# State-space decay: exponents from products with a selecting operand, or loaded from DRAM onto all partitions

## The chip, the cores and the metric

One NeuronCore of a Trainium2 chip runs the whole kernel. The metric is the device time of one execution in microseconds (us); the median of several runs counts. Five engines work side by side and wait for each other by semaphores: PE (TensorE, matrix products and transposes into PSUM banks), DVE (VectorE), ACT (ScalarE), POOL (GpSimd) and SP (SyncE, which here only issues DMAs). All data is float32; "fp32r" is the same width in the form that TensorE takes for its rounded products.

## The reference

One inference step of a hybrid decoder layer: a sliding-window attention branch and a Mamba-2 state-space (SSD) branch side by side, an output projection, and a squared-ReLU MLP. There are 1024 prompt tokens with 16 meta tokens ahead of them, and 8 sample sequences of 4 tokens. What matters here is the decay inside the SSD scan (8 heads, chunks of 128 tokens):

```python
acum = jnp.cumsum((dt * a).reshape(b, nc, chunk, H), axis=2)
seg = acum[:, :, :, None, :] - acum[:, :, None, :, :]
decay = jnp.exp(jnp.where(causal, seg, -jnp.inf))
g = jnp.einsum('bcthn,bcshn->bctsh', ch, bh) * decay
y_diag = jnp.einsum('bctsh,bcshp->bcthp', g, xdt)
...
y_off = jnp.einsum('bclhn,bchpn->bclhp', ch, h_in) * jnp.exp(acum)[..., None]
```

For each chunk and head a 128 x 128 matrix of differences of the running exponent `acum` is needed (token t against token s), and its exponential; and `exp(acum)` of every token once more, as a factor of the part that comes from the carried state.

## The kernel before

The tokens are cut into nine blocks `i`: block 0 has 48 tokens (32 sample, 16 meta), blocks 1 to 8 have 128. The kernel runs in stages.

*Projections and attention.* The input projection's GEMMs run as a stream of slots; generators for the attention blocks and for `steps` (softplus, the running sums) are woven in between. `steps` (lines 816 to 861) leaves in SBUF `dt`, `te`, `ex` and `A4`. `A4` holds for each token and head the running exponent `acum` split into a rounded part `Ah` and a remainder, and the same two negated: 32 columns a block.

*The SSD stage with the first half of the output projection.* `interleave` advances a GEMM stream (`wout_stream`: 24 slots of 12 products for the attention half, then 16 slots for the mixer half) and, ahead of each slot's GEMM, every live generator by one `yield`. Each GEMM slot loads a piece of the residual input into `hb` (three buffers, line 993), adds the product's PSUM bank `g` (three banks) to it on VectorE (line 996), and stores it to `hd` (line 997). Block i's `mixer(i)` starts at slot round(2.25 i), block 5 at slot 12. The order of the instructions on each engine's queue is that of the framework's scheduler, which need not be the written one.

In that stage `exponents` (line 924) runs once for block 0, once for blocks 1 to 4 and once for 5 to 8. It transposes `A4` (line 927), and VectorE and ScalarE build from it `L` (line 945), `R` (line 941, with the constant `delta`) and `Tr` (line 947), so that a product over 32 rows of the contraction yields `acum[t] - acum[s]`. `ssd(i)` (line 1041) then makes the decay like this:

```python
pd = ptile()
mm(pd[:M, :4 * M], L[:, :M], R[:, 4 * g:4 * g + 4, :M], True, True)
...
eA = sp.tile([128, 4, M], F32, name="eA", tag="eA" + z, bufs=nb)
pe = ptile()
for j in range(4):
    mm(pe[:, j * M:j * M + M], sl[:, j, :], Tr[:, :M], True, True)
```

`pd` has the differences of four heads in one PSUM bank (512 columns), for each of two groups `g`; ScalarE clamps (Relu, line 1074) and takes the exponential (line 1075), VectorE multiplies by the masked product `Gm` (line 1076) into `Mt`. `pe` spreads `acum` over the partitions of each head by the selecting constant `selr` (loaded by POOL, line 920); its exponential is `eA` (line 1081), which later scales the carried state's part (lines 1108 and 1111) and, for block 0, the sample states. All the small products of the stage take turns in three PSUM banks named `s`; `y` and `f` have one each. In the profile a product in an `s` bank with the operands `R,L` is a `pd`, one with `Tr,selr` a `pe`.

In a chunk the steps come in this order: transposes and `Gm` in the first slot; the decay in the second; nothing in the third; in the fourth the products with `Mt` (`y`), the new state (`hn`), the carried part (`f`, with `eA`); then `gate`, which loads `zt`, normalises and writes the operand of the mixer half.

*After it.* The rest of the output projection, the MLP's two products and the final norms, mostly TensorE work. All products go through the helper on line 204.

Of the kernel before, what the change touches and what calls it, by code (L numbers as in the profile page):

```python
# [20 lines left out]
NT = 9  # L21
# [29 lines left out]
def _consts():  # L51
# [22 lines left out]
    delta = np.zeros((128, 8))  # L74
    mm = np.zeros((128, 2))
    sel = np.zeros((128, 4, 128))
    for r in range(128):
        k = r % 32
        delta[r, k % 8] = 1
        if k < 16:  # L80
            for j in range(4):
                for hh in range(2):
                    if k % 8 == 2 * j + hh:
                        sel[r, j, hh * 64:hh * 64 + 64] = 1
            mm[r] = (0, 1)
        else:
            mm[r] = (1, 0)
    put("delta", delta)
    put("mm", mm)
    put("seqm", np.tile(np.kron(np.eye(8), np.ones((4, 1))), (3, 1)))  # L90
    resident = at[0]
    put("sel", sel.reshape(128, 512))
# [101 lines left out]
def body(ctx: ExitStack, tc: tile.TileContext, xT, xm, win, wdt, wo, wu, wd, ck, cv, sc, st, sT, vec, consts,  # L194
# [162 lines left out]
    A4 = xp.tile([128, NT, 32], F32, name="A4")  # L357
# [458 lines left out]
    def steps():  # L816
# [34 lines left out]
        Ah = pa.tile([128, NT, 8], F32R, name="Ah")  # L851
        Ac = pa.tile([128, NT, 8], F32, name="Ac")
        for rows, s in ((128, slice(1, NT)), (48, slice(0, 1))):
            DVE.tensor_copy(out=Ac[:rows, s], in_=acum[:rows, s])
            ACT.copy(out=Ah[:rows, s], in_=acum[:rows, s])
            DVE.tensor_tensor(out=te[:rows, s], in0=tot[:rows, s], in1=Ac[:rows, s], op=ALU.subtract)
            ACT.activation(out=ex[:rows, s], in_=tot[:rows, s], func=AF.Exp)
            ACT.activation(out=te[:rows, s], in_=te[:rows, s], func=AF.Exp)
            DVE.tensor_copy(out=A4[:rows, s, 0:8], in_=f(Ah[:rows, s]))
            DVE.tensor_tensor(out=A4[:rows, s, 8:16], in0=Ac[:rows, s], in1=f(Ah[:rows, s]), op=ALU.subtract)  # L860
            DVE.tensor_scalar(out=A4[:rows, s, 16:32], in0=A4[:rows, s, 0:16], scalar1=-1.0, scalar2=None, op0=ALU.mult)

# [58 lines left out]
    mmc = c("mm")  # L921
    LR = {}

    def exponents(rows, w, s):
        n = w // 32
        tp = ptile()
        PE.transpose(tp[:w, :rows], A4[:rows, s, :], ident[:rows, :rows])
        if n > 1:
            L = sp.tile([128, 4, 128], F32R, name="L", tag="L", bufs=1)
            Tr = sp.tile([128, 4, 128], F32R, name="Tr", tag="Tr", bufs=1)  # L930
            R = sp.tile([128, 8, 128], F32R, name="R", tag="R", bufs=1)
            POOL.memset(f(L), 0.0)
            POOL.memset(f(Tr), 0.0)
        else:
            L = sp.tile([128, 1, T0], F32R, name="L0")
            Tr = sp.tile([128, 1, T0], F32R, name="Tr0")
            R = sp.tile([128, 8, 128], F32R, name="R0", tag="Bm", bufs=1)
        tm = sp.tile([128, 128], F32, name="tm", tag="dg", bufs=2)
        DVE.tensor_scalar(out=tm[:w, :rows], in0=tp[:w, :rows], scalar1=mmc[:w, 1:2], scalar2=mmc[:w, 0:1], op0=ALU.mult, op1=ALU.add)
        for h in range(0, 8, 4):  # L940
            DVE.tensor_tensor(out=R[:w, h:h + 4, :rows], in0=tm[:w, :rows].unsqueeze(1).broadcast_to([w, 4, rows]),
                              in1=c("delta", w)[:, h:h + 4].unsqueeze(2).broadcast_to([w, 4, rows]), op=ALU.mult)
        for q in range(n):
            rr = slice(32 * q, 32 * q + 32)
            DVE.tensor_scalar(out=L[rr, q, :rows], in0=tp[rr, :rows], scalar1=mmc[rr, 0:1], scalar2=mmc[rr, 1:2],
                              op0=ALU.mult, op1=ALU.add)
            ACT.copy(out=Tr[rr, q, :rows], in_=tp[rr, :rows])
        for q, i in enumerate(range(s.start, s.stop)):
            LR[i] = (L[:w, q], R[:w], Tr[:w, q], selr[:w])


# [89 lines left out]
    def ssd(i):  # L1041
        r0, M = TOK[i]
        X_, B_, C_ = xcols(i)
        L, R, Tr, sl = LR[i]
# [24 lines left out]
        for g in range(2):  # L1069
            pd = ptile()  # L1070
            mm(pd[:M, :4 * M], L[:, :M], R[:, 4 * g:4 * g + 4, :M], True, True)

            mt = Mt[:M, g, :, :M]
            ACT.activation(out=mt, in_=pd[:M, :4 * M].rearrange("p (r t) -> p r t", r=4), func=AF.Relu, scale=-1.0)
            ACT.activation(out=mt, in_=mt, func=AF.Exp, scale=-1.0)
            DVE.tensor_tensor(out=mt, in0=mt, in1=Gm[:M, g, :M].unsqueeze(1).broadcast_to([M, 4, M]), op=ALU.mult)
        eA = sp.tile([128, 4, M], F32, name="eA", tag="eA" + z, bufs=nb)
        pe = ptile()
        for j in range(4):
            mm(pe[:, j * M:j * M + M], sl[:, j, :], Tr[:, :M], True, True)  # L1080
        ACT.activation(out=eA, in_=pe[:, :4 * M].rearrange("p (j t) -> p j t", j=4), func=AF.Exp)
# [116 lines left out]
    def decays(i):  # L1198
# [3 lines left out]
    def mixer(i):  # L1202
        if i == 0:
            yield from decays(i)
# [662 lines left out]
```

## Time and profile before

| | |
|---|---|
| median of 3 runs | 1129.27 us (1129.19 to 1129.62) |
| the profiled execution | span 1128.1 us from its first to its last instruction; its own device time is not given apart from that, and the median lies 1.2 us above the span |
| TensorE busy | 1110.9 us (98%) |
| VectorE / ScalarE / GpSimd busy | 838.3 / 569.6 / 223.5 us (74 / 50 / 20%) |
| DMA | 177.64 MB, mean 157 GB/s |
| granted TensorE clock in the SSD stage | 1.00 |

A busy TensorE is not TensorE at its peak: matmuls are pipelined, and each one's duration runs into the next. What a product costs is therefore read from the start of one to the start of the next. In a group's row stand the line, engine, operation, out <- in, shapes and count, then the busy us in total, the mean ns of one, and the idle time of the engine just before them with what ended it. "us to landing" of a DMA is from its issue to its last byte's arrival.

### The profile page before, as it was taken

Reading aid. Unit: us, or ns where it says so; the run is one execution under the profiler, and the core shown is the slowest. Engines: PE = TensorE matmul, PEld = TensorE weight load, DVE = VectorE, ACT = ScalarE, POOL = GpSimd, SP = SyncE. Lnnn points to the kernel's source line nnn. Section 1 sums busy time; section 2 is a strip of 40 time slices with the busy share of each in tenths; the row PEclk is TensorE's granted clock in tenths of the full one; section 3 lists DMA queues with packets and bytes.
Section 4 is the critical chain, followed back from the end, with each engine's and each line's share of the span. In section 5 each row is a group of like instructions: output and inputs, shape, how many; then the busy total and the mean of one; then the engine's idle time right before and its main releaser. Section 6 shows DMA issues by size and latency. Waiting matters only on the chain.

```text
span 1128.1 us, 21791 instructions
## 1 busy us (share of the span) xinstructions
PE 1110.9 (98%) x8403; PEld 1072.7 (95%) x8403; DVE 838.3 (74%) x1624; ACT 569.6 (50%) x1205; POOL 223.5 (20%) x291
## 2 busy tenths in 40 slices
PE   8999999999999999999999999999999999999997
PEld 8989988889888899999999999999999999999997
DVE  6646888985788968998877777766599656867483
ACT  8312467575675748854444444444434334546361
POOL 0442365664344441210000000000000000000001
PEclk9999999999999999999999999999999999999999
DMA  8131100111466476666653443524999654465273
GB/s 287 70 98 38 38 24 34 38 53 42 144 211 196 142 268 219 211 191 216 211 190 106 162 153 134 178 90 170 384 307 322 191 172 109 118 197 169 76 229 111
DMA packets 84424, 177.64 MB, mean 157 GB/s; under 512 B 10692, under 2 KB 32740, under 8 KB 82272
## 3 DMA queue, kind: packets, MB, share of 16 engines
q1 hardware_dynamic: 77392, 141.59, 40.2%
q0 software_dynamic: 6224, 33.74, 7.5%
q8 instruction: 66, 1.08, 0.4%
q10 hardware_dynamic: 704, 0.92, 0.2%
q14 instruction: 38, 0.31, 0.1%
HBM read 125.49 MB, written 50.72 MB: 156 GB/s over the span
## 4 chain that ended last, share of the span: by engine, by line
PE 77%; DVE 10%; ACT 5%; issue 3%; DMA 3%; POOL 1%; POOLq 0%; SPq 0%; ACTq 0%; DVEq 0%
PE g L204 42%; PE b L204 19%; PE c L204 9%; PE s L204 3%; PE o L204 1%; ACT p L681 1%; DMA wraw<-in_win 1%; DVE Qs L712 1%; PE y L204 1%; DMA wdr<-in_wd 1%; DMA wraw<-in_wo 1%; DVE Sd L1612 1%; PE pt L745 1%; DVE p L679 1%; DVE bc L526 1%
## 5 line engine op out<-in xcount | busy, mean ns | idle before, releaser
L204 PE MATMUL g<-acth,whi 128*128 128x384 f32 (+2 forms) x528 | 161.9, 331 | 0.2 <-DVE qT L456 0.2
L204 PE MATMUL g<-acth,wlo 128*128 128x384 f32 (+2 forms) x528 | 159.3, 327 | 1.2 <-DVE hb L996 1.2
L204 PE MATMUL g<-actl,whi 128*128 128x384 f32 (+2 forms) x432 | 140.6, 325 | 0.0
L1625 ACT CAST ts<-tr 128x528 fp32r<-128x528 f32 x92 | 58.2, 632 | 119.2 <-PE b L204 99.2
L1626 DVE TENSOR_TENSOR ts<-tr,ts 128x528 fp32r<-128x528 f32 x92 | 64.9, 705 | 54.5 <-ACT ts L1625 53.8
L204 PEld LDWEIGHTS g<-acth,whi 128*128 128x128 f32 x528 | 97.3, 188 | 2.1 <-issue 1.0
L204 PEld LDWEIGHTS g<-acth,wlo 128*128 128x128 f32 x528 | 97.1, 188 | 1.5 <-DVE hb L996 1.3
L204 PEld LDWEIGHTS g<-actl,whi 128*128 128x128 f32 x432 | 81.4, 189 | 0.1
L323 POOL TENSOR_TENSOR rs<-rs,nhalf 128x3 f32<-128x3 f32 x9 | 10.4, 1153 | 334.5 <-DMA wdq<-in_wd 285.5
L1341 ACT COPY s<-g 128x264 f32<-128x264 f32 x90 | 33.9, 377 | 62.0 <-PE g L204 61.5
L236 POOL TENSOR_TENSOR wlo<-wraw,whi 128x256 fp32r<-128x256 f32 x56 | 50.0, 924 | 11.8 <-ACT whi L233 11.6
L1414 POOL DMA_DIRECT2D u<-u x16 | 8.5, 533 | 177.0 <-ACT u L1357 147.2
L1346 DVE TENSOR_TENSOR u<-b,s 128x264 f32<-128x264 f32 x64 | 27.4, 429 | 19.5 <-PE b L204 10.1
L735 POOL TENSOR_TENSOR p<-p,sm 128x512 f32<-128x512 f32 (+1 forms) x32 | 34.3, 1093 | 31.4 <-DVE sm L733 29.6
L1351 ACT ACTIVATE u<-u 128x528 f32<-128x528 f32 x42 | 27.1, 646 | 26.4 <-DVE u L1350 26.4
L204 PE MATMUL b<-ts,w7y 128*128 128x264 f32 x279 | 39.3, 285 | 0.0
L204 PE MATMUL g<-ts,whi 128*128 128x264 f32 x279 | 38.9, 284 | 0.0
L204 PE MATMUL g<-ts,w7y 128*128 128x264 f32 x279 | 38.9, 283 | 0.0
L204 PE MATMUL b<-ts,whi 128*128 128x264 f32 x279 | 38.9, 284 | 0.0
L204 PE MATMUL g<-ts,wlo 128*128 128x264 f32 x270 | 38.0, 285 | 0.0
L204 PE MATMUL b<-ts,wlo 128*128 128x264 f32 x270 | 37.3, 282 | 0.0
L681 ACT ACTIVATE p<-p,nm 128x257 f32<-128x257 f32 (+1 forms) x64 | 31.3, 492 | 11.0 <-DVE nm L679 10.8
(584 smaller groups left out, 3475.7 us busy)
## 6 DMA issues: line engine op xcount, KB each, us to landing
tr<-u SPq DMA_DIRECT2D x92, 264.0 KB, 3.1
wraw<-in_wu SPq DMA_DIRECT2D x38, 512.0 KB, 4.0
wdr<-in_wd SPq DMA_DIRECT2D x68, 256.0 KB, 4.0
u<-t POOLq DMA_DIRECT2D x16, 1056.0 KB, 5.6
wraw<-in_win SPq DMA_DIRECT2D x16, 512.0 KB, 3.7
u<-u POOLq DMA_DIRECT2D x10, 792.0 KB, 3.6
wraw<-in_wo SPq DMA_DIRECT2D x24, 256.0 KB, 2.9
h<-he SPq DMA_DIRECT2D x16, 264.0 KB, 5.2
```

Source lines behind the costliest of these rows:

```text
L204: PE.matmul(out, lhsT=a, rhs=b, start=start, stop=stop, skip_group_check=on)
L236: eng.tensor_tensor(out=lo[:, n], in0=raw[:, n], in1=f(hi[:, n]), op=ALU.subtract)
L526: DVE.scalar_tensor_tensor(out=acc, in0=cb[:, j:j + CL], scalar=cw_(j), in1=acc, op0=ALU.mult, op1=ALU.add)
L679: DVE.tensor_tensor_reduce(out=s_out[:, 0:W], in0=ps, in1=mask, scale=-scale, scalar=nsink, op0=ALU.add, op1=ALU.min, accum_out=nm)
L681: ACT.activation(out=s_out[:, 0:W + 1], in_=s_out[:, 0:W + 1], func=AF.Exp, bias=nm, scale=-1.0, accum_out=sm)
L712: DVE.tensor_tensor(out=Q[oth, g, :, :rows], in0=src, in1=f(Q[own, g, :, :rows]), op=ALU.subtract)
L735: POOL.tensor_tensor(out=p[:rows, r:r + 2, :W], in0=p[:rows, r:r + 2, :W], in1=sm[:rows, r:r + 2].unsqueeze(2).broadcast_to([rows, 2, W]), ...
L1341: ACT.copy(out=s[:, c], in_=ps[c][:, :TQ])
L1346: DVE.tensor_tensor(out=out[:, c], in0=ps[c][:, :TQ], in1=s[:, c], op=ALU.add)
L1351: ACT.activation(out=x, in_=x, func=AF.Square)
L1625: ACT.copy(out=t[:, 0], in_=x)
L1626: DVE.tensor_tensor(out=t[:, 1], in0=x, in1=f(t[:, 0]), op=ALU.subtract)
```

## The change

`exponents` with its operands `L`, `R`, `Tr` and the constants `delta`, `mm` and `sel` go. `steps` now keeps `Ac` (acum as it is, tokens on partitions), transposes it once, and writes two small tables to DRAM: `ad` = -acum and `ed` = exp(acum), one row of 128 tokens for each block and head. For each block a generator `decays(i)`, started two slots ahead of `ssd(i)`, loads `ad`'s eight rows onto all partitions (`Ab`, two buffers) and `ed`'s rows onto the two halves of the partitions (`eA`, two buffers). `ssd(i)` then forms the clamped differences head by head: four on VectorE (add a per-partition scalar, then max with 0) and four on ScalarE (Relu with a per-partition bias), one exponential over all eight heads, and one product with `Gm`. All times of `mixer(i)` stay.

```diff
-    A4 = xp.tile([128, NT, 32], F32, name="A4")
+    Ac = xp.tile([128, NT, 8], F32, name="Ac")
+    ad = dram.tile([NT * 8, 128], F32, name="ad")
+    ed = dram.tile([NT * 8, 128], F32, name="ed")
...
-        Ah = pa.tile([128, NT, 8], F32R, name="Ah")
-        Ac = pa.tile([128, NT, 8], F32, name="Ac")
+        POOL.memset(Ac[:, 0], 0.0)
         for rows, s in ((128, slice(1, NT)), (48, slice(0, 1))):
             DVE.tensor_copy(out=Ac[:rows, s], in_=acum[:rows, s])
-            ACT.copy(out=Ah[:rows, s], in_=acum[:rows, s])
...
-            DVE.tensor_copy(out=A4[:rows, s, 0:8], in_=f(Ah[:rows, s]))
-            DVE.tensor_tensor(out=A4[:rows, s, 8:16], in0=Ac[:rows, s], in1=f(Ah[:rows, s]), op=ALU.subtract)
-            DVE.tensor_scalar(out=A4[:rows, s, 16:32], in0=A4[:rows, s, 0:16], scalar1=-1.0, scalar2=None, op0=ALU.mult)
+        yield
+
+        tp = ps_tile("o")
+        PE.transpose(tp[:F9, 0:128], Ac.rearrange("p i h -> p (i h)"), ident)
+        for n, (dst, func, sign) in enumerate(((ad, AF.Copy, -1.0), (ed, AF.Exp, 1.0))):
+            t = pa.tile([F9, 128], F32, name=f"At{n}")
+            ACT.activation(out=t, in_=tp[:F9, 0:128], func=func, scale=sign)
+            SP.dma_start(out=dst, in_=t)
...
-    selr = sp.tile([128, 4, 128], F32R, name="selr")
-    a, b = CCOL["sel"]
-    POOL.dma_start(out=selr.rearrange("p j q -> p (j q)"), in_=consts[:, a:b])
...
+    def decays(i):
+
+        M = TOK[i][1]
+        z = "0" if i == 0 else ""
+        Ab = sp.tile([128, 8, M], F32, name="Ab", tag="Ab" + z, bufs=1 if i == 0 else 2)
+        SP.dma_start(out=Ab[:M], in_=ad[8 * i:8 * i + 8, 0:M].unsqueeze(0).broadcast_to([M, 8, M]))
+        eA = sp.tile([128, 4, M], F32, name="eA", tag="eA" + z, bufs=1 if i == 0 else 2)
+        for hh in range(2):
+            src = ed[8 * i:8 * i + 8, 0:M].rearrange("(j q) t -> q j t", q=2)[hh]
+            SP.dma_start(out=eA[HALF[hh]], in_=src.unsqueeze(0).broadcast_to([64, 4, M]))
+        DEC[i] = Ab, eA
+        yield
...
-        for g in range(2):
-            pd = ptile()
-            mm(pd[:M, :4 * M], L[:, :M], R[:, 4 * g:4 * g + 4, :M], True, True)
-
-            mt = Mt[:M, g, :, :M]
-            ACT.activation(out=mt, in_=pd[:M, :4 * M].rearrange("p (r t) -> p r t", r=4), func=AF.Relu, scale=-1.0)
-            ACT.activation(out=mt, in_=mt, func=AF.Exp, scale=-1.0)
-            DVE.tensor_tensor(out=mt, in0=mt, in1=Gm[:M, g, :M].unsqueeze(1).broadcast_to([M, 4, M]), op=ALU.mult)
-        eA = sp.tile([128, 4, M], F32, name="eA", tag="eA" + z, bufs=nb)
-        pe = ptile()
-        for j in range(4):
-            mm(pe[:, j * M:j * M + M], sl[:, j, :], Tr[:, :M], True, True)
-        ACT.activation(out=eA, in_=pe[:, :4 * M].rearrange("p (j t) -> p j t", j=4), func=AF.Exp)
+        mt = Mt[:M, :, :, :M]
+        for h in range(8):
+            e, a = Mt[:M, h // 4, h % 4, :M], Ac[:M, i, h:h + 1]
+            if h < 4:
+                DVE.tensor_scalar(out=e, in0=Ab[:M, h], scalar1=a, scalar2=0.0, op0=ALU.add, op1=ALU.max)
+            else:
+                ACT.activation(out=e, in_=Ab[:M, h], func=AF.Relu, bias=a)
+        ACT.activation(out=mt, in_=mt, func=AF.Exp, scale=-1.0)
+        DVE.tensor_tensor(out=mt, in0=mt, in1=Gm[:M, :, :M].unsqueeze(2).broadcast_to([M, 2, 4, M]), op=ALU.mult)
...
-    interleave(wout_stream(), [(12 if i == 5 else round(2.25 * i), mixer(i)) for i in range(NT)] +
-               [(1, decays(1)), (10, decays(5))])
+    interleave(wout_stream(), [(max(0, at_slot(i) - 2), decays(i)) for i in range(NT)] +
+               [(at_slot(i), ssd(i)) for i in range(NT)])
```

More of the change, by code (lines that the diff above doesn't have):

```diff
@@ L916, in body @@
     ppt = w3.enter_context(pool("ppt", space=PSUM))
-    selr = sp.tile([128, 4, 128], F32R, name="selr")
-    a, b = CCOL["sel"]
-    POOL.dma_start(out=selr.rearrange("p j q -> p (j q)"), in_=consts[:, a:b])
[L921 to L949, printed above, removed]
@@ new lines, in body @@
+    DEC = {}
+    def decays(i):
[9 more added lines that the diff above has]
+        yield
@@ L1043, in ssd @@
         X_, B_, C_ = xcols(i)
[L1044 removed]
+        Ab, eA = DEC.pop(i)
         z = "0" if i == 0 else ""
```

26 lines of the change are left out of this document (2 added, 24 removed).

## The prediction

> **What bounds the kernel now.** I read the page first (busy shares, then the chain that ended last), then the stage that the change edits: its busy times by stretch, TensorE's instructions in order of time, TensorE's waits, the groups by line, the SyncE queue.
>
> ```profile
> PE 1110.9 (98%) x8403; PEld 1072.7 (95%) x8403; DVE 838.3 (74%) x1624; ACT 569.6 (50%) x1205; POOL 223.5 (20%) x291
> PE 77%; DVE 10%; ACT 5%; issue 3%; DMA 3%; POOL 1%; POOLq 0%; SPq 0%; ACTq 0%; DVEq 0%
> 300.00:412.00 112.00, 108.70 (x814) 95.26 (x813) 96.59 (x214) 71.62 (x181) 47.85 (x47) 1.00 0.63 192
> 300.00:305.00 5.00, 4.56 (x32) 3.59 (x30) 3.80 (x9) 3.75 (x11) 1.28 (x3) 1.00 1.05 341
> 350.00:360.00 10.00, 9.29 (x70) 8.25 (x70) 9.76 (x20) 3.84 (x12) 5.14 (x4) 1.00 0.78 236
> 380.00:400.00 20.00, 19.63 (x142) 17.46 (x141) 18.56 (x41) 12.02 (x28) 9.82 (x10) 1.00 0.47 144
> ...
> PE g L204 <- DVE hb L996: 1.2, 1, 1.2
> PE s L1049 <- ACT Tr L947: 0.7, 1, 0.7
> PE s L1051 <- ACT eA L1081: 0.4, 2, 0.2
> PE s L204 <- ACT eA L1081: 0.2, 1, 0.2
> ```
>
> TensorE is busy for 98% of the span and makes 77% of the chain. The third row is the edited stage (the nine `ssd` chunks beside the output projection's GEMMs); after the duration come the busy us of PE, PEld, DVE, ACT, POOL, then the granted clock, the DMA share and GB/s. TensorE is busy 108.7 of 112 us, and its named waits there are short: the longest four, shown, add up to 2.5 us. So TensorE sets this stage, and a product that leaves it should shorten it. VectorE is the runner-up, with 96.59 of 112 us (0.86); in the stretch 380 to 400 it reaches 0.93, in 350 to 360 0.98. That is the second limit, and near. In the first 5 us the DMA engines are full (share 1.05, 341 GB/s).
>
> **The change, part by part.** TensorE loses, for each chunk, two exponent products (`pd`, 512 columns) and four selecting products (`pe`, 128 columns):
>
> ```profile
> 306.46 0.29 PE L204 MATMUL s<-R,L 32*48 32x192 f32 x1
> 306.59 0.53 PE L204 MATMUL s<-Tr,selr 32*128 32x48 f32 x4
> 307.06 0.62 PE L204 MATMUL g<-acth,wlo 128*128 128x384 f32 x2
> ...
> 311.15 0.39 PE L204 MATMUL s<-R,L 128*128 128x512 f32 x1
> 311.39 0.51 PE L204 MATMUL g<-acth,whi 128*128 128x384 f32 x2
> 311.79 0.51 PE L204 MATMUL s<-R,L 128*128 128x512 f32 x1
> 312.13 0.56 PE L204 MATMUL s<-Tr,selr 128*128 128x128 f32 x4
> 312.62 1.13 PE L204 MATMUL s<-xw,Bt 16*128 16x256 f32 x4
> ...
> 319.51 0.71 PE L204 MATMUL s<-R,L 128*128 128x512 f32 x2
> 320.06 0.56 PE L204 MATMUL s<-Tr,selr 128*128 128x128 f32 x4
> 320.45 0.39 PE L204 MATMUL g<-acth,wlo 128*128 128x384 f32 x1
> ```
>
> Matmuls overlap, so the price is from start to next start, not the duration. Chunk 1: 311.39 - 311.15, plus 312.62 - 311.79, is 1.07 us. Chunk 2: 320.45 - 319.51 is 0.94. I take 1.0 for each of the eight full chunks: 8.0 us. The narrow chunk 0: 0.60 for its second product and its selection, and 0.13 (306.59 - 306.46) again for its first: 0.7. Three transposes in `exponents` go and one in `steps` comes; a net two, estimated at the selecting products' pitch of 0.10 us (0.39 / 4), are 0.2. TensorE: 8.9 us less. The waits on `Tr` and `eA` (1.3 us) should go as well, since a chunk takes three turns less of the three `s` banks; but as another wait may take their place I count nothing for them and keep 1.3 for the lower end.
>
> VectorE and ScalarE:
>
> ```profile
> L1076 DVE TENSOR_TENSOR Mt<-Mt,Gm 128x512 f32<-128x512 f32 x16 | 10.7, 684 | 1.3 <-ACT Mt L1075 1.3
> L945 DVE TENSOR_SCALAR L<-s,cs 32x128 fp32r<-32x128 f32 x8 | 3.2, 405 | 0.5 <-ACT Tr L947 0.4
> L941 DVE TENSOR_TENSOR R<-tm,cs 128x512 fp32r<-128x512 f32 x4 | 2.5, 671 | 0.0
> L369 DVE TENSOR_TENSOR sqy<-sqy 128x256 f32<-128x256 f32 x8 | 3.4, 420 | 1.2 <-ACT sqy L1188 1.2
> L1668 DVE TENSOR_SCALAR dg<-cs,rs 128x128 f32<-128x128 f32 x11 | 2.6, 280 | 1.7 <-POOL rs L1784 0.9 <-POOL rs L323 0.8
> L861 DVE TENSOR_SCALAR A<-A 128x128 f32<-128x128 f32 x1 | 0.2, 209 | 0.0
> L1055 ACT ACTIVATE xs<-xs,vec 128x128 f32<-128x128 f32 x32 | 10.5, 401 | 0.7 <-PE s L1049 0.7
> L1075 ACT ACTIVATE Mt<-Mt 128x512 f32<-128x512 f32 x16 | 9.4, 627 | 0.0
> L1074 ACT ACTIVATE Mt<-s 128x512 f32<-128x512 f32 x16 | 8.9, 593 | 6.9 <-PE s L204 6.7
> L1081 ACT ACTIVATE eA<-s 128x512 f32<-128x512 f32 x8 | 4.7, 590 | 0.0
> L1639 ACT ACTIVATE q<-h 128x1024 f32<-128x1024 f32 x1 | 1.0, 1043 | 0.0
> ```
>
> VectorE loses `exponents`: 8 x 405 and 4 x 671 ns are 5.9 us; `tm` and chunk 0's narrow operations I estimate at 5 more by the 405 ns row, 2.0: 7.9 us. It gains 32 differences of 128x128 from SBUF with a per-partition scalar. L1668 is that operation at that size: 280 ns; L861, the same without a pointer operand, 209, is the lower bound, and 405 (from PSUM) the upper. I take 280, the nearest: 9.0 us, and 0.8 for chunk 0. The closing product becomes one of 1024 columns; 256 more columns cost 264 ns (684 - 420), so it takes 684 + 2 x 264 = 1212 for 2 x 684: eight times 0.16, 1.3 us less. Net: 9.8 - 7.9 - 1.3 = +0.6 us, 97.2 in the stage (94.9 by 209 ns, 101 by 405). ScalarE per chunk loses 2 x 593, 2 x 627 and 590 ns and gains 4 x 401 (a Relu with a per-partition bias; L1055 has a per-partition scale) and 1043: 0.4 us less, and the engine has 40 us idle; I count nothing.
>
> So TensorE would let the stage shrink by 8.9 us to 103, and VectorE would then be 0.94 busy. At the 0.93 that it holds for 20 us, 97.2 us of work need 104.5: the gain is capped at 7.5 us. (At 0.98 no cap; at today's 0.86, 113 us: nothing gained.) I take 0.93, the longest stretch of high load.
>
> The loads. Each full chunk adds 512 KB (`Ab`) and 256 KB (`eA`) in three issues on SyncE's queue, chunk 0 some 170 KB; `selr` (256 KB) goes.
>
> ```profile
> 297.85 0.94 SPq L242 DMA_DIRECT2D wraw<-in_wo  x2
> 298.92 0.34 SPq L668 DMA_DIRECT2D zd<-thz  x1
> 299.31 1.51 SPq L993 DMA_DIRECT2D hb<-in_xm  x3
> 300.92 0.51 SPq L1133 DMA_DIRECT2D st<-in_st  x1
> 305.88 0.33 SPq L997 DMA_DIRECT2D hd<-hb  x1
> ...
> 299.31 6.07 DMA hb<-in_xm
> ...
> hb<-in_xm SPq DMA_DIRECT2D x16, 192.0 KB, 3.1
> st<-in_st SPq DMA_DIRECT2D x4, 512.0 KB, 5.1
> ```
>
> At the start they hurt: `hb` of the first GEMM takes 6.07 us and ends TensorE's longest wait (1.2 us, above). Chunks 0 and 1 load there too: 0.94 MB more, 0.26 less, at 341 GB/s 2.0 us. Lower bound 0 (issued behind `hb`, or earlier, before 298.92, while the queue waits for `thz`), upper 2.8 (all 0.94 MB ahead of `hb`). I take 2.0, as written order puts them first. [...]
>
> Later loads I cost at nothing. They are issued two slots ahead; 24 GEMM slots in the stage's 112 us make 4.7 us a slot, so some 9 us of cover for landings of 3 to 5 us. The stage's 192 GB/s at share 0.63 become about 0.83 with 6.3 MB more. If the cover goes, `Mt` is late and TensorE waits before `y`. Nor do I count 27 issues of 0.3 to 0.5 us on the queue. In `steps`, ScalarE and VectorE swap operations of about 0.2 us (L861 is one) for a transpose, two activations and two stores while TensorE is at the projections; who waits behind those stores on SyncE is a weight load that is prefetched. Nothing, within 0.5 us each way.
>
> The sum: 7.5 - 2.0 = 5.5 us less than the span of 1128.1, so 1122.6; the runs' median, 1129.27, lies 1.2 above that span, which gives **1123.8 us**.
>
> **The rivals.** *A: VectorE does not cap.* If a narrow difference takes L861's 209 ns, VectorE has 94.9 us, at 0.93 102: TensorE's 8.9 passes whole, with the 1.3 us of bank waits, and if the start's loads are hidden the time is 1129.3 - 10.2 = 1119.1. For it: the waits are really on banks that come free. Against: the pointer operand is in the 280 ns row. [...]
>
> *B: VectorE is the bound already.* If its 0.86 is what its chains allow, 97.2 us need 113, and the 8.9 us come back as TensorE's waits on `Mt`, `xd` and `hb`: 1129.3 to 1130.3. For it: it is the stage's second engine by 12 us, and the differences of a chunk (4 x 280, beside 4 x 401 on ScalarE) stand ahead of one 1043 ns exponential where today two halves pipeline. Against: today TensorE waits on it for some 2 us only.
>
> *C, slower: loads that wait for their buffer hold SyncE's queue.* `eA` has two buffers; that of chunk i-2 is last read three slots after its `ssd` began, which is the slot in which chunk i asks for it (one later for chunks 7 and 8). If the queue stands there, the next `hb` load stands behind it, lands 3.1 us late, and VectorE, in order, waits before its sum, and then TensorE for a `g` bank. Six chunks at 3.1 less what the slot's GEMM covers (12 x 0.17 = 2.0), so 1.1 to 3.1 each: 6.6 to 18.6 us, 1130 to 1142, about 1136. It decides from 0.9 us a chunk (5.5 / 6). Against: three `hb` loads and `st` were issued ahead of the first `hd` store that stands before them in the code, so the queue is ordered by readiness.
>
> **How the numbers follow.** Forecast 0.47 (1121 to 1127); A 0.18; B 0.20; C 0.15. Faster by over 0.2% (2.3 us, about what a measurement tells from no change): forecast and A, 0.65; within it: B, 0.20; slower: C, 0.15. The range goes from below A (1118.0) to the lower edge of C (1131.5): it leaves out most of C and a little of A.
>
> **What would show it.** Right: no `R`, `L` or `Tr` groups on TensorE, and its starts in the stage close up by about 1 us a chunk; differences near 280 ns; the closing product near 1.2 us; VectorE at 0.93 in the stage. The start's step: `hb` landing after 306 us and a longer TensorE wait on it. A: VectorE under 0.92 and TensorE without waits. B: TensorE's waits on `Mt`, `xd` and `hb` sum to 7 us or more. C: SyncE's waits at the `eA` loads, then VectorE's on `hb`. I am wrong altogether if a broadcast load of one 4 KB row to 128 partitions lands far later than a plain one of its size; no row here shows such a load.

## The result: 1 per cent slower

The changed kernel takes 1141.16 us (median of 4 runs, 1140.76 to 1141.88) against 1129.23 for the kernel before in the same job (1128.82 to 1129.62). The ratio is 1.0103, interval 1.0089 to 1.0117: by the ratio, slower by 11.6 us (10.0 to 13.2), where 5.5 us less was forecast, and outside the range given. The profiled execution has a span of 1140.1 us and a time of 1141.88, 1.8 above it.

The page of the changed kernel, its busy line and its chain:

```profile
PE 1109.3 (97%) x8347; PEld 1072.9 (94%) x8347; DVE 843.2 (74%) x1627; ACT 564.8 (50%) x1196; POOL 219.6 (19%) x287
PE 73%; DVE 11%; DMA 6%; ACT 4%; issue 3%; POOL 1%; SPq 1%; POOLq 0%; DVEq 0%; ACTq 0%
```

The edited stage of the changed kernel by stretch (columns as in the prediction: start:end, duration, busy us of PE, PEld, DVE, ACT, POOL, granted clock, DMA share, GB/s):

```profile
310.00:315.00 5.00, 0.79 (x6) 0.69 (x3) 4.94 (x10) 3.25 (x10) 2.92 (x2) 0.83 0.05 15
315.00:320.00 5.00, 5.00 (x17) 5.00 (x17) 3.93 (x9) 2.81 (x8) 0.02 (x1) 0.50 0.79 256
380.00:400.00 20.00, 18.90 (x137) 16.59 (x136) 18.94 (x39) 10.93 (x30) 9.18 (x9) 1.00 0.80 244
412.00:424.00 12.00, 7.60 (x42) 7.18 (x43) 6.84 (x18) 4.14 (x10) 4.81 (x6) 0.94 0.94 289
300.00:424.00 124.00, 107.33 (x773) 95.21 (x772) 104.37 (x228) 67.41 (x175) 47.16 (x45) 0.95 0.77 236
```

The same 124 us of the kernel before:

```profile
300.00:424.00 124.00, 120.70 (x892) 107.26 (x891) 102.33 (x227) 76.52 (x191) 52.74 (x52) 1.00 0.67 211
```

TensorE has 56 instructions fewer, so the products did go (nine blocks of 2 + 4, three transposes, one new). But it stands idle 16.7 of these 124 us where it had 3.3, and part of its busy time runs at half the clock (0.50 in 315 to 320). In the chain TensorE lost 4 points and DMA gained 3. Two places stand out: 310 to 320, the start of the stage, and 412 to 424, the passage from the attention half to the mixer half.

The steps of the stage show when the loss arises. `hb` sums are VectorE's additions of a GEMM's bank to the residual (line 996 before, 965 after), 24 of them; then come the sums of the mixer half. Their start times, read from the two traces: the second sum 308.3 before, 314.2 after; the 24th 406.3 and 413.5; the second `hb` sum of the mixer half 411.7 and 423.1. What follows that last one, to the end of the program, took 716.4 us before and 717.0 after (714.2 to 721.0 in the kernels of the experiments). So nearly the whole loss of the change lies inside the stage: about 6 us at its start, still 7 at the 24th sum, 11 at the mixer half.

The chain says the same by engine. From 300 to 425 us its pieces on TensorE add up to 83 us before and 23 after, those on VectorE to 17 and 45, the transfers to 6 and 34.

**The start.** SyncE's timeline in the changed kernel (start, duration, engine, line, operation, tiles):

```profile
300.04 0.42 SPq L913 DMA_DIRECT2D Ab<-ad  x1
300.52 1.30 SPq L917 DMA_DIRECT2D eA<-ed  x2
301.92 0.55 SPq L913 DMA_DIRECT2D Ab<-ad  x1
302.57 1.77 SPq L917 DMA_DIRECT2D eA<-ed  x2
304.39 1.08 SPq L962 DMA_DIRECT2D hb<-in_xm  x2
```

Six issues of the new loads stand ahead of the first `hb` load, which went out at 299.31 before and goes out at 304.39 now. VectorE's, GpSimd's and TensorE's timelines of the same kernel (in brackets the idle time before and its releaser):

```profile
310.98 2.32 DVE L1042 TENSOR_SCALAR Mt<-Ab,Ac 128x128 f32<-128x128 f32 x3
313.21 0.68 DVE L1029 TENSOR_TENSOR xd<-s,dt 128x512 f32<-128x512 f32 x1
313.81 0.91 DVE L965 TENSOR_TENSOR hb<-hb,g 128x288 f32<-128x288 f32 x2
```

```profile
311.12 1.90 POOL L1109 TENSOR_TENSOR Bm<-BS,cs 96x1024 fp32r<-96x1024 f32 x1 [2.33 <-ACT Mt L1044]
```

```profile
314.31 0.69 PE L187 MATMUL g<-acth,wlo 128*128 128x384 f32 x1 [4.21 <-DVE hb L965]
...
315.11 0.84 PE L187 MATMUL g<-acth,wlo 128*128 128x384 f32 x2
```

While `hb` is under way, VectorE takes up the differences of blocks 0 and 1, and the `hb` sum comes behind them in its order. The first five `hb` loads took 5.5 us at most to land, so the first was there before 310; its sum began at 313.81. One of these differences takes 1.92 us instead of 0.28: it begins 0.06 us after GpSimd's `Bm` and ends 0.09 us after it. TensorE waits 4.21 us for a `g` bank. Then the products of 384 columns start 0.32 us apart until past 318 (clock 0.50), where a `g` product cost 0.17 in the prediction. In the changed kernel the granted clock stood at 0.50 in three places of the stage, 314 to 320, 375 to 378 and 423 to 425, each with one of TensorE's three longest idle times at it or shortly ahead of it: 4.21, 2.20 and 3.26 us, which end at 314.31, 372.27 and 421.31. Its other idle times in the stage, 1.07 us at most, have no such place behind them, and in the kernel before, where the longest is 1.15, the stage has clock 1.00. What sets the clock is not shown.

**Later.** SyncE's timeline in the changed kernel again, at a place that recurs:

```profile
341.27 0.32 SPq L966 DMA_DIRECT2D hd<-hb  x1
341.64 1.77 SPq L917 DMA_DIRECT2D eA<-ed  x2
343.46 0.60 SPq L962 DMA_DIRECT2D hb<-in_xm  x1
```

The waits of the changed kernel from 298 to 425, of TensorE, VectorE and SyncE in turn (who, line, for what, line: us in total, times, longest):

```profile
PE g L187 <- DVE hb L965: 5.3, 2, 4.2
...
PE g L187 <- DVE hb L940: 3.3, 1, 3.3
...
DVE hb L965 <- DMA hb<-in_xm: 4.2, 4, 1.9
...
DVE hb L940 <- DMA hb<-hd: 3.0, 1, 3.0
...
SPq L966 <- DVE hb L965: 31.9, 16, 7.6
...
SPq L917 <- DVE hn L1064: 3.6, 1, 3.6
SPq L917 <- DVE rsb L305: 3.2, 1, 3.2
...
SPq L917 <- PE s L1018: 1.1, 1, 1.1
```

The `eA` loads wait on SyncE (7.9 us in the last three rows: the first two for their buffer, the third at the start). The first of SyncE's rows is larger. An `hd` store stands on SyncE until VectorE has made its sum, 31.9 us in 16 waits (38.4 us with the rows that name another instruction of VectorE; 25.7 in the kernel before), and what stands behind it, the next `hb` load included, goes out only then. The `hb` loads of the kernel before waited 21.7 us for the landing of earlier stores, whose buffers they take; that wait is 4.5 us now. At 341.64, and again at 356.09 and 376.99, issues of `eA` stand between such a store and the `hb` load; the chain runs through this place three times. The transfers take longer too (the issues from 300 to 424: size, median us to landing; the kernel after, then before, then pieces of the chain after):

```profile
Ab<-ad SPq DMA_DIRECT2D x8, 512.0 KB, 5.4
...
hb<-in_xm SPq DMA_DIRECT2D x16, 192.0 KB, 4.4
hd<-hb SPq DMA_DIRECT2D x16, 192.0 KB, 3.2
eA<-ed SPq DMA_DIRECT2D x16, 128.0 KB, 3.7
```

```profile
hb<-in_xm SPq DMA_DIRECT2D x16, 192.0 KB, 3.1
hd<-hb SPq DMA_DIRECT2D x16, 192.0 KB, 2.6
```

```profile
343.46 3.73 DMA hb<-in_xm
...
356.71 4.80 DMA hb<-in_xm
...
377.63 4.78 DMA hb<-in_xm
...
414.44 6.27 DMA hb<-hd
```

The last of these pieces is the passage: the first `hb` of the mixer half is loaded back from `hd` at 414.44, behind two `ha` loads, and lands at 420.7. Before, the same load went out at 404.92, ahead of them.

**VectorE's differences**, and what ScalarE's exponential waited for (group rows of the kernel after; then the spread of one line, min/median/max in ns):

```profile
L1042 DVE TENSOR_SCALAR Mt<-Ab,Ac 128x128 f32<-128x128 f32 x32 | 13.0, 446 | 0.1
L1046 DVE TENSOR_TENSOR Mt<-Mt,Gm 128x1024 f32<-128x1024 f32 x8 | 10.0, 1252 | 1.2 <-ACT Mt L1045 1.1
L1045 ACT ACTIVATE Mt<-Mt 128x1024 f32<-128x1024 f32 x8 | 8.4, 1054 | 9.8 <-DVE Mt L1042 9.8
```

```profile
L1042 DVE TENSOR_SCALAR Mt<-Ab,Ac x36: 230/276/1920, 305.8 to 400.7; 128x128 f32<-128x128 f32 x32, 48x48 f32<-48x48 f32 x4
```

The median is 276 ns as forecast (280), the mean 446: some of them stand while a GpSimd instruction runs. (The 13.0 us of the row count overlapping operations once, so they are less than 32 x 446 ns.) ScalarE sat idle 9.8 us before its exponential, waiting for them; in the chain from 300 to 425 the differences themselves make 7.4 us.

### The profile page after: what moved, and what is told of

It is laid out like the page before. It is cut to its first block, busy times and chain, and to the rows that moved or that the text cites. A ratio compares the mean times of both kernels' runs of the same rounds, so it can differ in the third digit from the quotient of the medians.

```text
span 1140.1 us, 21717 instructions
## 1 busy us (share of the span) xinstructions
PE 1109.3 (97%) x8347; PEld 1072.9 (94%) x8347; DVE 843.2 (74%) x1627; ACT 564.8 (50%) x1196; POOL 219.6 (19%) x287
## 4 chain that ended last, share of the span: by engine, by line
PE 73%; DVE 11%; DMA 6%; ACT 4%; issue 3%; POOL 1%; SPq 1%; POOLq 0%; DVEq 0%; ACTq 0%
PE g L187 42%; PE b L187 18%; PE c L187 9%; DMA wdr<-in_wd 2%; PE s L187 2%; DMA hb<-in_xm 1%; PE o L187 1%; ACT p L666 1%; DMA wraw<-in_win 1%; DVE Qs L697 1%; DVE Mt L1042 1%; DVE ts L1585 1%; PE pt L730 1%; DVE p L664 1%; DVE hb L965 1%
## 5 line engine op out<-in xcount | busy, mean ns | idle before, releaser
L187 PE MATMUL g<-acth,wlo 128*128 128x384 f32 (+2 forms) x528 | 162.2, 333 | 7.6 <-DVE hb L965 4.2
L187 PEld LDWEIGHTS g<-acth,wlo 128*128 128x128 f32 x528 | 99.5, 193 | 9.0 <-DVE hb L965 5.2
```

The costliest lines, as they stand in the source:

```text
L187: PE.matmul(out, lhsT=a, rhs=b, start=start, stop=stop, skip_group_check=on)
```

## The experiments

Each kernel was timed beside the kernel before on the same chip, so the ratios are compared, not the times; "us over before" is (ratio - 1) x 1129.2. The last column is the start of the second `hb` sum, a mark of what the stage's start cost (308.3 before). lead1, hb4 and act8_pool_queue rest on two runs each, the others on three to ten.

The framework's scheduler orders each engine's queue anew for every kernel, and this bears on what a gain shows. From 295 to 430 us VectorE has 236 instructions in the changed kernel. `ea_rows` has them in the same order, `hb4` and `ea3` all but 2 and 4; in `lead1` 43 stand elsewhere in the order, in `small_ea`, `pool_queue`, `small_ab` and `ea_pool` 58 to 69, in `load_once` 59 of 220 (counted in the traces: the fewest that would have to move). Where the order changed, a gain can come from it as well as from what the edit names. No run here cuts the bytes and keeps the order.

| kernel | ratio (interval) | us over before | second sum |
|---|---|---|---|
| the change | 1.0103 (1.0089 to 1.0117) | 11.6 | 314.2 |
| lead1 | 1.0113 (1.0071 to 1.0155) | 12.8 | 314.0 |
| pool_queue | 1.0055 (1.0031 to 1.0078) | 6.2 | 307.4 |
| ea_pool | 1.0074 (1.0059 to 1.0089) | 8.4 | 311.5 |
| ea3 | 1.0080 (1.0062 to 1.0099) | 9.0 | 314.2 |
| hb4 | 1.0115 (1.0085 to 1.0144) | 13.0 | 313.5 |
| load_once | 1.0034 (1.0022 to 1.0047) | 3.8 | 313.7 |
| small_ab | 1.0013 (0.9998 to 1.0027) | 1.5 | 310.6 |
| small_ea | 1.0044 (1.0029 to 1.0059) | 5.0 | 313.2 |
| ea_rows | 1.0105 (1.0088 to 1.0121) | 11.9 | 313.9 |
| act8 | 1.0043 (1.0029 to 1.0057) | 4.9 | 312.1 |
| act8_small | 0.9962 (0.9949 to 0.9976) | -4.3 | 310.2 |
| act8_pool_queue | 1.0113 (1.0084 to 1.0143) | 12.8 | 305.6 |
| act8_hb4 | 1.0035 (0.9998 to 1.0073) | 4.0 | 311.9 |
| act8_hb4_lead1 | 1.0049 (1.0027 to 1.0072) | 5.5 | 312.4 |
| act8_ea_rows | 1.0054 (1.0039 to 1.0069) | 6.1 | 312.1 |
| ea_only | 1.0011 (1.0000 to 1.0023) | 1.2 | 308.8 |
| ab_only | 1.0027 (1.0008 to 1.0047) | 3.0 | 308.7 |
| ab_only_act8 | 0.9979 (0.9969 to 0.9988) | -2.4 | 306.6 |

### Where the loads stand in the queues

**lead1**: the loads one slot ahead of `ssd` instead of two.

```diff
-    interleave(wout_stream(), [(max(0, at_slot(i) - 2), decays(i)) for i in range(NT)] +
+    interleave(wout_stream(), [(max(0, at_slot(i) - 1), decays(i)) for i in range(NT)] +
```

> The changed kernel with each chunk's loads started one slot ahead of its ssd instead of two, so that at the start only chunk 0's small loads stand ahead of the first hb load. Theory S (the start: six loads ahead of hb on SyncE's queue cost the first hb sum about 8 us, and TensorE's idle time there halves its clock for some 3 us): the first hb sum at 309 us or earlier instead of 313.8, no stretch at half clock near 315, time 1132 to 1136. Theory P (the narrow differences on VectorE wait for GpSimd through the whole stage) and theory D (6 MB more of loads slow hb and zt all along): at most 2 us better, 1139 to 1142.

No gain. The first sum came at 307.1, but the second at 314.0: the stall moved behind it. The clock at 315 to 320 was 0.50 again.

**pool_queue**: all three loads of a block from GpSimd's queue. **ea_pool**: only the two `eA` loads.

```diff
-        SP.dma_start(out=Ab[:M], ...)
+        POOL.dma_start(out=Ab[:M], ...)
...
-            SP.dma_start(out=eA[HALF[hh]], ...)
+            POOL.dma_start(out=eA[HALF[hh]], ...)
```

> The changed kernel with the Ab and eA loads issued from GpSimd's queue instead of SyncE's: the same bytes and the same buffers, but no hb, hd or zt stands behind them on SyncE. Theory Q: the first hb load goes out at 299 to 300 again and the time falls by 6 to 9 us, 1132 to 1135. Theory B: within 2 us of the changed kernel, 1139 to 1142; GpSimd's 27 issues of 0.5 to 0.8 us could add to that.

> The changed kernel with only the two eA loads of a chunk on GpSimd's queue; Ab stays with SyncE. Theory Q: the issues and buffer waits of eA leave the queue in which hb stands, and 5 to 7 us come back, all that moving both queues gave (1135 to 1137), or more, since Ab's landing is not delayed. Theory B: bytes are unchanged, 1140 to 1142.

With both moved, half of the loss goes (11.6 to 6.2), and the start is whole (307.4). What is left is later: the landing of the `hd` stores goes from 3.2 to 5.2 us, of `zt` from 4.2 to 5.4, of `Ab` from 5.4 to 6.9. The twelfth `hb` sum still comes at 352.3 (352.9 in the kernel before), the 24th at 407.5 (406.3) and the second of the mixer half at 416.8 (411.7), so most of what is left arises in the passage. With `eA` alone moved, 3 us come back. Taking the loads out of SyncE's queue helps the start and does not make them free.

**ea3**: a third buffer for `eA`, so that its loads need not wait on SyncE.

```diff
-        eA = sp.tile([128, 4, M], F32, name="eA", tag="eA" + z, bufs=1 if i == 0 else 2)
+        eA = sp.tile([128, 4, M], F32, name="eA", tag="eA" + z, bufs=1 if i == 0 else 3)
```

> The changed kernel with three buffers for eA instead of two, so that chunk i's eA loads need not wait until chunk i-2 has used its copy. Theory Q (the wait of the eA loads holds SyncE's queue, and the hb load behind them is late): SyncE's waits at the eA loads on hn, rsb and s, 7.9 us after the change, go, and with them 4 to 8 us: 1133 to 1137. Theory B (the bytes of the two loads make the landings longer, whatever the queue does): the same waits go but the hb landing stays at 4.4 us and the time at 1141, within 1.5.

SyncE's waits at the `eA` loads on `hn` and `rsb` are gone, only 1.2 us on `s` and 1.4 on `Ab`'s landing are left, but the time fell by 2.6 us by the ratios, and the intervals overlap. The buffer wait that rival C was built on is not the main part.

**hb4**: a fourth `hb` buffer, so that the `hb` load need not wait for the store of an earlier one.

```diff
-            hb = sp.tile([128, 384], F32, name="hb", tag="hb", bufs=3)[:, :cw]
+            hb = sp.tile([128, 384], F32, name="hb", tag="hb", bufs=4)[:, :cw]
...
```

> The changed kernel with four hb buffers instead of three (1.5 KB a partition more). Theory B, in the form that the added bytes lengthen each turn of the hb ring (load, sum, store, and only then the next load into that buffer), and VectorE and a g bank wait for the ring: a fourth buffer covers it, 1133 to 1137. If the bytes hurt elsewhere (Ab late for its own differences, zt, sT) or VectorE's own time binds: 1139 to 1142.

Nothing: the number of `hb` buffers is not the limit. This agrees with SyncE's rows above, where the `hb` loads of the changed kernel stand behind a store and wait little for a buffer. With the differences on ScalarE (below), and with one slot of lead as well, it is nothing again.

> All differences on ScalarE and four hb buffers, everything computed. If the two costs add as they did for act8_small: 1126 to 1130, level with the kernel before or a little under it. If the ring is not where the bytes hurt: as act8, 1133 to 1135.

> act8_hb4 with the loads one slot ahead instead of two, so that at the start only chunk 0's loads precede the first hb load. If the start then passes without the halved clock: 2 to 4 us less than act8_hb4, 1123 to 1127. If, as in lead1, VectorE's order and the second hb load bring the same stall a slot later: within 1.5 us of act8_hb4.

### How much is loaded

**load_once**: `Ab` and `eA` are loaded for blocks 0 and 1 alone and used for all (the scaled state then goes into a tile of its own, since `eA` has to keep its content). **small_ab**: one of `Ab`'s eight rows is loaded (64 KB for 512) and used for all heads; issues and waits stay. **small_ea**: one of `eA`'s four head pairs.

```diff
+        if i > 1:
+            DEC[i] = DEC[1]
+            return
...
```

```diff
-        SP.dma_start(out=Ab[:M], in_=ad[8 * i:8 * i + 8, 0:M].unsqueeze(0).broadcast_to([M, 8, M]))
+        SP.dma_start(out=Ab[:M, 0:1], in_=ad[8 * i:8 * i + 1, 0:M].unsqueeze(0).broadcast_to([M, 1, M]))
...
```

```diff
-            SP.dma_start(out=eA[HALF[hh]], in_=src.unsqueeze(0).broadcast_to([64, 4, M]))
+            js = slice(0 if i == 0 else 3, 4)
+            SP.dma_start(out=eA[HALF[hh]][:, js], in_=src[js].unsqueeze(0).broadcast_to([64, 4 if i == 0 else 1, M]))
...
```

> The changed kernel with Ab and eA loaded for chunks 0 and 1 only; chunks 2 to 8 take chunk 1's tables again, so their decay is left out as a computation of their own, with the same instructions on every engine but 21 loads (5.4 MB) less. Theory D: 1130 to 1134. Theories S and P: the start and the differences are as they were, so 1138 to 1141.

> The changed kernel with Ab's load cut to one head's row (64 KB a chunk instead of 512; all differences read that row, so seven heads' decay is left out). Every issue, every wait for a buffer and every instruction stays; only bytes go (about 3.7 of 6.3 MB). Theory B (bytes: the loads take DMA time from hb, zt and hd): most of the 9 us that load_once got back, so 1133 to 1136. Theory Q (queue: eA and Ab loads stand on SyncE's queue ahead of hb, waiting for their buffers and taking 0.4 to 0.6 us each to issue): 1139 to 1141, since the queue is as it was.

> The changed kernel with eA's loads of the full chunks cut to one of four head pairs (64 KB for 256 a chunk), which the product with the carried state then uses for all; the scale of the other head pairs is thereby left out. Ab whole, all issues and waits stay. Theory B by proportion: Ab's cut of 448 KB a chunk gave 10.8 us, so 192 KB give 4.6: 1136.5. Theory B with a limit (only the sum of both loads is too much, as each alone cost 1 to 4 us): nearly all of it, 1131 to 1134. Theory Ab alone (its bytes, not eA's, do the harm): 1141.

All three give most of the loss back: 7.8, 10.1 and 6.6 us by the ratios. `load_once` shows, whatever the mechanism, that the later loads cost 7.8 us. `small_ab` keeps in its code every issue, buffer and wait of the change and takes away 448 KB a chunk; in its chain from 300 to 425 us the transfers make 11 us instead of 34, VectorE 38 instead of 45. So what the DMAs carry probably costs more than their number, but this is not shown alone, since the order changed too: in `small_ab` the first `hb` sum stands on VectorE behind three of block 1's four differences, in the changed kernel behind all four and an `xd`. `small_ea` takes away 192 KB; in proportion to `small_ab` that would be 4.3 us, and the intervals are too wide to tell 6.6 from it. `load_once` has the late start in full (313.7, clock 0.51 at 315 to 320), yet by the twelfth sum it is within 1.6 us of the kernel before (354.5 against 352.9): a late start is made up again where the later loads are missing. The change, at that sum, is 13 us behind (366.0).

**ea_rows**: `ed`'s rows stored in another order, so that an `eA` load reads 2 KB in one piece for each partition instead of four pieces of 512 B; the bytes stay.

```diff
-            src = ed[8 * i:8 * i + 8, 0:M].rearrange("(j q) t -> q j t", q=2)[hh]
+            src = ed[8 * i + 4 * hh:8 * i + 4 * hh + 4, 0:M]
...
```

> The changed kernel with the rows of ed stored in another order, so that each half's four rows of a chunk stand together in DRAM: an eA load then reads 2 KB in one piece for each partition instead of four pieces of 512 B (one more store early in the kernel). Bytes, issues and waits stay. Small pieces: if the number of pieces is what eA's loads cost, most of the 6.3 us that the cut to a quarter of eA gave comes back: 1135 to 1137, and hb's landing falls from 4.4 towards 4.2 us. Bytes: nothing, 1140 to 1142.

> The same order of ed's rows, with all eight differences on ScalarE. Small pieces: 1134.0 less 4 to 6, 1128 to 1130, about as before the change. Bytes: 1133 to 1135.

No difference in either. So it is not the pieces; in `ea_rows` the order of every engine is that of the change as well. One reading falls with it: `hb`'s median landing here was 3.2 us instead of 4.4, and the time did not move. The landing of the 192 KB `hb` loads alone is thus not the measure of the loss.

### The differences on VectorE

**act8**: all eight differences of a chunk on ScalarE.

```diff
-            if h < 4:
+            if h < 0:
```

> The changed kernel with all eight differences of a chunk on ScalarE, none on VectorE. Theory P: VectorE's busy time in the stage falls by some 14 us (32 x 446 ns and 4 x 444), its long waits beside GpSimd's operations shrink from 14 us to about 8, and the time falls to 1130 to 1134. Theory S: the loads at the start stay, so the first hb sum still comes at 309 to 312 and the time is 1136 to 1140. Theory D: 1138 to 1141.

6.7 us come back. ScalarE's exponential no longer waits for VectorE (the row of the kernel act8 that answers to L1045 above):

```profile
L1044 ACT ACTIVATE Mt<-Ab,Ac 128x128 f32<-128x128 f32 x64 | 20.2, 388 | 1.0 <-DMA Ab<-ad 1.0
L1045 ACT ACTIVATE Mt<-Mt 128x1024 f32<-128x1024 f32 x8 | 8.4, 1055 | 0.1
```

ScalarE takes 32 more of 388 ns, 12.4 us, and VectorE is rid of 14.5 (13.0 and the narrow ones of block 0). The order on VectorE changed here too. VectorE was the tighter engine: 18.94 of 20 us at 380 to 400 after the change, while ScalarE had 10.93.

**act8_small** (with `small_ab`) and **act8_pool_queue** (with `pool_queue`):

> All differences on ScalarE, and Ab's load cut to one head's row (seven heads' decay left out). Theory B with VectorE as the second cost: 7 and 5 us come back, 1128 to 1131. Theory Q: as act8, 1133 to 1135.

> Both at once: all differences on ScalarE, the loads issued from GpSimd's queue. If the two costs are separate (VectorE's narrow operations 7 us by act8, the queue 6 to 9 us) the time is 1126 to 1128, a little under the kernel before. If both hide the same wait (VectorE's sums of hb come late either way), 1131 to 1134.

The first adds the two gains almost in full (15.9 of 16.8 us) and is 4.3 us faster than the kernel before. The second shows that the two remedies that keep the bytes do not add: together they are as slow as the change, although the start is early (305.6). There TensorE waits for `Mt` and VectorE for `hb` (two rows of the waits of act8_pool_queue, 298 to 425):

```profile
PE y L187 <- DVE Mt L1046: 8.9, 2, 8.0
```

```profile
DVE hb L965 <- DMA hb<-in_xm: 11.4, 2, 8.6
```

One `hb` load of 192 KB, issued from SyncE at 318.53, took 11.2 us to land there. `Ab`'s 512 KB, issued from GpSimd at 320.15, took 8.6 and were there before it; the DMA engines were full meanwhile (share 1.03, 378 GB/s from 320 to 325). So with loads on two queues the small urgent one landed last here. Why it struck this kernel and not `pool_queue` is not shown.

### Each half of the change alone

**ea_only**: the kernel before, with `eA` loaded (one slot ahead, not two) and the `pd` products kept. **ab_only**: the kernel before, with the differences from `Ab` and `eA` still by products (and in one buffer, not two). **ab_only_act8**: the same with all differences on ScalarE.

```diff
-        eA = sp.tile([128, 4, M], F32, name="eA", tag="eA" + z, bufs=nb)
-        pe = ptile()
-        for j in range(4):
-            mm(pe[:, j * M:j * M + M], sl[:, j, :], Tr[:, :M], True, True)
-        ACT.activation(out=eA, in_=pe[:, :4 * M].rearrange("p (j t) -> p j t", j=4), func=AF.Exp)
+        eA = DEC.pop(i)
```

```diff
-        for g in range(2):
-            pd = ptile()
-            mm(pd[:M, :4 * M], L[:, :M], R[:, 4 * g:4 * g + 4, :M], True, True)
...
+        for h in range(8):
+            e, a = Mt[:M, h // 4, h % 4, :M], Ac[:M, i, h:h + 1]
+            if h < 4:
+                DVE.tensor_scalar(out=e, in0=Ab[:M, h], scalar1=a, scalar2=0.0, op0=ALU.add, op1=ALU.max)
+            else:
+                ACT.activation(out=e, in_=Ab[:M, h], func=AF.Relu, bias=a)
...
```

> The kernel before with one part of the change: exp(acum) comes from DRAM into eA (256 KB a chunk, one slot ahead), so that the selecting products, Tr and selr go; the exponent products pd with L and R stay, and so do ScalarE's two Relus and two exponentials. TensorE loses about 0.4 us a chunk, 3.6 us. Theories S and P: nothing of what hurt is here, so 1125 to 1127. Theory D (any added load slows hb): 1128 to 1131.

> The other part of the change alone: the differences from Ab (512 KB a chunk) by VectorE and ScalarE, while eA still comes from the selecting products with Tr and selr. (To fit, Ab has two buffers over all nine chunks and eA one.) Theory B, with costs in proportion to the bytes and the differences on VectorE and ScalarE here whole: 1138 to 1142, the whole loss, since ea_only lost 1 us only. If the loss needs both loads at once: 1130 to 1134.

> The kernel before with the differences from Ab, all eight on ScalarE, and eA still by TensorE's products, so only 512 KB a chunk in one issue are added, and VectorE loses its four differences a chunk. If the 7 us of VectorE's differences are paid here as well as with both loads: 1132.9 - 7 = 1126, faster than before. If they come out only where the loads already hold VectorE up: near 1131 to 1133. Half way, 1129, is no difference from before.

`ea_only` takes some 3.6 us of products from TensorE (the selecting ones, 0.49 us in chunk 1 and 0.39 in chunk 2 by the starts that the prediction shows) and gives none of it back as time. `ab_only` costs 3.0. The two alone make 4.2, together 11.6; of the 7.4 between them, 5 are there at the second sum already (0.5 and 0.4 us late alone, 5.9 together). With both, six issues and 0.94 MB stand ahead of the first `hb` load; alone, it is two issues of `eA` or two of `Ab`. That this alone makes the 5 us is not tested. That the start can be made up again (`load_once`) forbids adding this 5 to the end as it stands.

`ab_only_act8` is the version with everything computed that beats both kernels: 1126.73 us (median of 10 runs; the profiled execution is the slowest of them, 1128.9), 2.4 us (1.4 to 3.5) under the kernel before. Moving the differences to ScalarE gave 5.4 us here, and 6.7 with both loads: this cost does not hang on `eA`'s loads. Three views of it answer to those of the change above: SyncE's timeline at the start, TensorE's longest waits, and the stage as one stretch.

```profile
298.99 1.08 SPq L953 DMA_DIRECT2D Ab<-ad  x2
300.11 2.07 SPq L999 DMA_DIRECT2D hb<-in_xm  x3
```

```profile
PE s L204 <- DVE Gm L1072: 1.0, 2, 0.7
PE s L204 <- DVE st L1184: 0.8, 1, 0.8
```

```profile
300.00:424.00 124.00, 118.58 (x896) 106.94 (x896) 100.50 (x206) 90.48 (x242) 57.03 (x49) 1.00 0.76 249
```

None of the longest waits is for `hb`, clock 1.00 throughout, at the same DMA share as the change (0.76 and 0.77) and a little more traffic (249 and 236 GB/s). The share alone does not tell which of the two is in trouble. From this kernel to act8 the main step is `eA` from DRAM for the selecting products, and it costs 7.3 us.

## Why the prediction was wrong

**TensorE's part was right and worth nothing.** The products are gone, at the price read from their starts. But the first paragraph's reading, that a product which leaves TensorE shortens the stage, failed: `ea_only` took 3.6 us from it for no gain. Whether `eA`'s 256 KB a chunk ate the gain or there was none is not told apart by that run; but with `Ab`'s bytes cut and the differences on ScalarE (`act8_small`) the same loss of products does come with 4.3 us less, near the 5.5 forecast, though that kernel differs in two more things. So TensorE sets the stage only as long as the loads and VectorE keep up, and here both fell behind.

**"Later loads I cost at nothing" is the step that failed most.** The cover of two slots was real for the loaded data: the chain of the change has no piece in which something waits for `Ab` or `eA` (act8's has two, 3.62 us for `eA` at 302.01 and 5.10 for `Ab` at 326.44). What had no cover was the other traffic. 768 KB a chunk take the same queue as the `hb` loads, the `hd` stores and `zt`, whose landings lie on the chain (29.17 of the 29.32 MB that moved from 300 to 424 went through it). Omitting the later loads gives 7.8 us back, so that is about the size of the term put at nothing; cutting `Ab`'s bytes gives 10.1. By which way the loads cost it (their bytes, their place on SyncE between a store and an `hb` load, or the order that the scheduler makes around them) is argued above and not separated. The prediction had the DMA share rise to 0.83 (its own terms give 0.81; 0.77 was measured, for 0.67) and drew nothing from it.

**The start's 2.0 us were 5.9 at the second sum.** I priced the bytes at 341 GB/s, with 2.8 as the upper end; the row that carried it was the right one (`hb` takes 6.07 us and ends the longest wait). Left out were the six issues on SyncE, some 4.3 us (300.04 to 304.39; "nor do I count 27 issues"), and that VectorE would take up the differences of two blocks first and reach the `hb` sum behind them (313.81), 3.8 us or more after the load had landed; then the half clock (0.50 in 315 to 320). The term's own weight in the end is less than 5.9, as `load_once` shows.

**VectorE's sum of +0.6 us was mis-sized, and so was what it means.** Closing product 1252 ns for 1212, differences 276 in the median for 280: the rows chosen were right. But the mean is 446, so 32 of them took 13.0 us for 9.0, because some of them stand while a GpSimd instruction runs (last section). And the differences can cost more than their sum, since ScalarE's one long exponential waits for them (9.8 us): rival B had said this, with two halves that pipeline today. Taking them off gave 6.7 and 5.4 us in two settings; how much of that is the hold and how much the wait is not separated.

**The rivals.** C had the side, the place and about the size (1136, upper end 1142), with 0.15; the range began to leave it out at 1131.5, though its own low end is 1130. Its rows came as foretold: SyncE's waits at the `eA` loads, then VectorE's on `hb`. Its mechanism was not the main one: with the buffer wait gone (`ea3`) 9.0 of 11.6 us remain. The argument against it, that the queue is ordered by readiness, did not help at 341.64, where `eA`'s issues went out first and `hb`'s 1.8 us behind them. B's signs came too: TensorE's waits on `hb` alone sum to 8.6 us. A fell: no full difference took less than 267 ns, and the cap was never reached. The warning that I would be wrong altogether if a broadcast load lands late did not come true: 512 KB from one 4 KB row land in 5.4 us, where `st`'s plain 512 KB took 5.1 before. The loads were as quick as hoped; they were late for others.

**What stays open.** The costs overlap: bytes 10, later loads 8, queue 5, VectorE's differences 7 of a loss of 12. By which transfer the bytes reach TensorE isn't settled: `hb`'s landing in the median doesn't follow the times (3.2 us in `ea_rows` with the loss in full, 4.2 in `small_ea` with more than half of it gone), and a fourth buffer changed nothing. The order of the queues, which changed in every kernel that gained more than 3 us, is a rival that no run leaves out; `lead1`, with another order and the same bytes, gained nothing. Nor is it shown why `eA`'s 256 KB cost 7.3 us beside `Ab` and 1.2 alone; the issues on SyncE (0.6 us each by the median, 18 in the stage) and the bytes both add there. A loading of `eA` as one DMA wasn't tried.

## What to carry to other kernels

A load that is issued early enough for its reader was still not free here (7.8 us came back without the later ones): price it by what it does to the small loads and stores whose landing a tight chain waits for, on its own queue and on others (with the new loads on GpSimd's queue the `hd` stores landed in 5.2 us for 3.2), and count the issues ahead of a stage's first urgent load (here six, 4.3 us). Before work is moved off the busiest engine, look at the second one by stretch, and put the replacement on the engine that has idle time there (here ScalarE at 55%, not VectorE at 95%, from 380 to 400 of the changed kernel). Try a change of two parts as two: here one half, with its differences on the idle engine, was faster, and the other half spoilt it. Where a scheduler orders the queues, compare the orders of two kernels before a gain is put down to the edit.

## What the hardware showed unexpectedly

VectorE's operations with SBUF sources were held while a GpSimd instruction ran: 1920 ns for 276, twice in the stage, each from under 0.1 us after `Bm` began to 0.09 after its end, and shorter holds behind other GpSimd instructions (1307 ns beside `whi`, 675 beside `xw`). Summing what VectorE's operations took above the lower quartile of their own form, where it was more than 0.05 us, 298 to 425: 5.6 us before, 14.3 after, 10.3 in `act8`, 7.2 in `ab_only_act8`. Not every one is held: of 35 in the changed kernel that began while a GpSimd instruction ran and read SBUF alone, 21 took longer; of 37 that read PSUM, none did, nor did any of the 159 that began while no GpSimd instruction ran. So moving work from a PSUM source to an SBUF source, as here, went with more of it (5.6 to 14.3 us). What decides which operation is held is not shown. The prediction left the holds out: its 280 ns row (L1668) has eleven operations, from 1077 to 1120 us, and none of them began while a GpSimd instruction ran.
